# Low weights by an adding transfer, casts on ScalarE and a select for the decay mask in a gated DeltaNet block

## The chip, the cores and the metric

The kernel runs on one core of one Trainium2 chip. The core has five engines that run side by side, each through its own queue in order: TensorE (PE, matrix products), VectorE (DVE), ScalarE (ACT), GpSimd (POOL) and SyncE (SP), which here issues all transfers. The metric is the device time of one execution in microseconds, the median of several; lower is better.

## The reference

One layer of a hybrid block. The input x has 1024 tokens of 1024 channels, and there are 256 context tokens that go through the same weights. Both are normalised and modulated, and one projection `w_in` gives the q, k, v, decay and beta columns of a gated DeltaNet with 8 heads, a gate z for it, and a pooling group with a gate of its own. Both groups are concatenated and go through `w_out`; the result is gated, added to x and normalised.

```
hn = rms_norm(x, gain) * (1 + scale) + shift
proj = hn @ w_in                       # q, k, v | decay, beta | z_dn | u_pool | z_pool
qkv = silu(short_conv(qkv, conv_w))    # 5 taps, centred
decay = exp(where(i >= s, g[i] - g[s], -inf))       # per head, direction and chunk
o_f, s_f = gated_delta_rule(q, k, v, g[0], beta[0], s0_f)      # and backward
o = rms_norm(o_f + flip(o_b)) * silu(z_dn)
y = concat(o, pool_mixer(u_pool) * pool_scale * silu(z_pool))
out = rms_norm(x + gate * (y @ w_out), final_gain)
```

The context is scanned first, and its final states are where the scans of x start. All data is float32.

## The kernel before

**Products in three passes.** TensorE multiplies a rounded format (`FP32R`). To keep float32 accuracy, each factor is split in a high part (a rounded copy) and a low part (the raw value minus the high part), and a product is the sum of high by high, high by low and low by high (`PASSES`, L724). So each tile of weights needs two tiles, `whi` and `wlo`, and each half of the normalised input needs `hnhi` and `hnlo`.

**The tiles of the projection.** `w_in` is worked through in 64 column tiles of 128 columns. A tile is loaded raw (512 KB, `w_load`, L669) into `wraw`, or in turn with a second buffer (tag `kT`) for the first 18 tiles. It is split in two halves of 128 x 512 (`w_split`, L679): ScalarE casts the high half, and GpSimd subtracts it from the raw half to give the low one. `gemm_half` (L734) runs 8 x 3 matmuls for 512 tokens (256 for the context) and, after a fixed number of them, places the split of the next tile and, for the later tiles, the load of the one after. `whi` and `wlo` have two buffers each.

**The stages.** The first 33 us compute the modulation from `w_mod`. Then come 16 context tiles (k and v of 8 heads, 256 columns of moving data each), while `x_half` (L1388) transposes, modulates and splits the input: TensorE transposes into PSUM, ScalarE writes `h32`, VectorE casts it to `hnhi`, and VectorE or GpSimd, in turn, subtracts for `hnlo` (`x_split`, L1408). After them the tiles of the heads (v, k, z, q), two early gates and the pooling columns follow. A tile of q, k or v goes through `conv_post` (L787) on VectorE: four steps for the outer taps, and one after a tanh on ScalarE.

**The jobs.** Two context jobs and eight head jobs go through threads: `stage_d` (L969) loads rows of cumulated decays broadcast over the partitions into the tile `D`, GpSimd adds a mask (0 or -1e30, one 128 x 128 tile per direction, made at the start at L533) and ScalarE takes the exponential. `stage_a` (L990) forms the products of keys, scales them by beta and the decay, and inverts 16 x 16 blocks on VectorE by way of two bounces through DRAM (`ds`, `vs`); `stage_b` merges the inverses, `stage_k`, `stage_q` and `stage_s` prepare the scan, and `scan_ctx` and `scan_x` run it.

**The order of the work.** It is fixed when the program is built, by a planner (`Flow`, L70). The main thread yields after each matmul; the planner keeps an estimated clock for every engine, and puts in a step of a side thread when its estimated due time has come. A thread also waits for flags, such as `("k", k)` when the convolution of a head's keys is written. The cost of each instruction comes from `Engine.cost` (L318), the gaps between engines from the table `AFTER`, and of a transfer from `ISSUE` and `LANDED` (L66). On the chip every engine then takes its instructions in that order and waits on semaphores.

**The end.** From 1023 us on the pooling columns are summed in windows on VectorE (`pool_mix`), split again and multiplied by `pool_w`, whose parts `load_all` (L1744) loads and splits group by group. `second_half` (L1969) frees the pooling tiles and loads the second half of `w_out` and of the mixed output `y`; `out_main` (L1829) contracts them.

Of the kernel before, what the change touches and what calls it, by code (L numbers as in the profile page):

```python
# [8 lines left out]
FP32 = mybir.dt.float32  # L9
# [56 lines left out]
ISSUE = 1220.0  # L66
LANDED = 950.0


# [244 lines left out]
class Engine:  # L314
# [3 lines left out]
    def cost(self, op, a, k):  # L318
# [24 lines left out]
        if op == "tensor_copy":  # L343
            return 80.0 + 3.8 * n
        if op == "memset":
            return 36.0 + 0.83 * n
# [12 lines left out]
    def __getattr__(self, op):  # L359
        f = getattr(self.real, op)  # L360

        def call(*a, **k):
            self.flow.spend(self.name, self.cost(op, a, k), self.uses(op, a, k))
            return f(*a, **k)  # L364

        return call


# [22 lines left out]
def kernel(  # L391
# [90 lines left out]
    ident = const.tile([P, P], FP32, name="ident")  # L482
    mask = [const.tile([P, P], FP32, name=f"mask{d}") for d in range(2)]
    tri = [dl_tile([P, P], "S", 2) for d in range(2)]
# [48 lines left out]
    for d in range(2):  # L533
        pool.memset(mask[d], 0.0)
        pool.memset(tri[d], 1.0)
        s = 1 if d == 0 else -1
        pool.affine_select(out=mask[d], in_=mask[d], pattern=[[s, P]], compare_op=ALU.is_ge, fill=NEG,
                           base=0, channel_multiplier=-s)
        pool.affine_select(out=tri[d], in_=tri[d], pattern=[[s, P]], compare_op=ALU.is_ge, fill=0.0,
                           base=0, channel_multiplier=-s)  # L540
# [138 lines left out]
    def w_split(n, part):  # L679
        if n >= len(order):  # L680
            return
        if part == 0:
            wq[n] = [gemm.tile([P, KT, P], FP32R, tag=f"w{s}", bufs=2, name=f"w{s}") for s in ("hi", "lo")]
        hi, lo = wq[n]
        s = slice(part * (KT // 2), (part + 1) * (KT // 2))
        split(raws[n][:, s, :], hi[:, s, :], lo[:, s, :], dve if n < WD and part else pool)

# [46 lines left out]
    def gemm_half(i, w, src, t0, m, evac):  # L734
        ps = mm_tile()
        j = 0
        for k in range(KT):
            for a, b in PASSES:
                pe.matmul(ps[:, 0:m], w[a][:, k, :], src(b, k, t0),
                          start=(j == 0), stop=(j == 3 * KT - 1))  # L740
                j += 1
                if t0 == 0 and j == (4 if i > 1 else 14) and i:
                    w_split(i + 1, 0)
                if t0 == 0 and j == (14 if i > 1 else 18) and i:
                    w_split(i + 1, 1)
                    if i + 2 >= N2:
                        w_load(i + 2)
                yield
        evac(ps[:, 0:m], t0)
# [219 lines left out]
    def stage_d(J, part):  # L969
# [9 lines left out]
        for d in range(2):  # L979
            pool.tensor_tensor(out=t[:, d], in0=t[:, d], in1=rep(mask[d], 4), op=ALU.add)  # L980
            if d or DY < 8:
# [406 lines left out]
    def x_half(hf):  # L1388
        for k in range(KT):
# [9 lines left out]
            if XACT & 4:  # L1399
# [3 lines left out]
                           scale=md[:, 0, 1, k:k + 1], bias=md[:, 0, 0, k:k + 1])  # L1403
            flow.give()
            flow.flag("h32", n)
            flow.add(x_split(hf, k, h32), [("h32", n)], True)

    def x_split(hf, k, h32):  # L1408
        if XACT & 8:
            yield "dve"  # L1410
        dve.tensor_copy(hn[2 * hf][:, k, :], h32)
        yield
        e = dve if k % XD == 0 else pool
# [70 lines left out]
    def thread_a():  # L1484
# [3 lines left out]
        for k in range(-2, H):  # L1488
            yield ("k", k)
            yield ("ab", k >= 0)  # L1490
            yield ("done", k - 2)
            yield from stage_a(jobs[k])

# [335 lines left out]
    def out_main():  # L1829
# [139 lines left out]
        def second_half():  # L1969
            yield ("mixed",)  # L1970
            pl_p.release()
            pools["c"] = Pool(flow, tc.alloc_tile_pool(name="outc", bufs=1, side="right", reuse_waits="tile"))
# [110 lines left out]
```

## Time and profile before

| | |
|---|---|
| median of 3 runs | 1318.51 us (1318.17 to 1319.07) |
| the profiled execution | 1321.76 us |
| its span, first to last instruction | 1320.0 us |
| TensorE matmul busy | 1212.5 us (92%) |
| VectorE busy | 928.0 us (70%) |
| ScalarE busy | 570.8 us (43%) |
| GpSimd busy | 438.7 us (33%) |
| granted TensorE clock, mean | 0.962 |
| moved by DMA | 123.73 MB |

Busy time is the share of the span in which an engine executes; issuing a transfer does not count as busy. A row of the profile names a line, and nearly all instructions share L364, the line of the recording helper, so rows are told apart by what they write and read: `wlo<-wraw,whi` is the subtraction that makes a low half from the raw and the high half. Behind the shapes stand the count, the busy time in us and the mean of one in ns.

### The profile page before, as it was taken

What the parts mean: (1) busy time and instruction counts of PE and PEld (TensorE: products, weight loads), DVE (VectorE), ACT (ScalarE), POOL (GpSimd) and SP (SyncE); (2) the same over time, 40 slices, a digit from 0 to 9 for tenths busy, and PEclk for the clock granted to TensorE, in tenths of its full rate; (3) what the DMA queues carried; (4) which work ended last, traced back from release to release, by engine and by line L of the source; (5) the groups of instructions that cost most, each with busy time, mean ns of one, the idle gap of its engine ahead of it and who ended that gap; (6) DMA issues with size and microseconds to landing.
All of it is one profiled execution on the core that took longest, in us unless ns stands there. A gap on an engine that the chain in (4) does not pass through costs nothing.

```text
span 1320.0 us, 26398 instructions
## 1 busy us (share of the span) xinstructions
PE 1212.5 (92%) x10631; PEld 977.8 (74%) x10631; DVE 928.0 (70%) x1883; ACT 570.8 (43%) x1498; POOL 438.7 (33%) x451
## 2 busy tenths in 40 slices
PE   8876699899899999999999989999999999799997
PEld 2666577677777877788778768778788777688887
DVE  4799989868886787877776867878433999724212
ACT  3466437444436547455474464643613123322110
POOL 2477433230421423314132233141215454402330
PEclk9788899899999999989999999999999899899999
DMA  9533344223121213212221131212313135565230
GB/s 329 188 99 93 86 140 125 74 57 90 37 49 48 78 42 100 58 46 80 49 83 44 41 100 41 69 63 43 103 60 109 48 104 185 199 206 157 83 112 32
DMA packets 157384, 123.73 MB, mean 94 GB/s; under 512 B 47106, under 2 KB 135115, under 8 KB 157261
## 3 DMA queue, kind: packets, MB, share of 16 engines
q1 hardware_dynamic: 157261, 122.04, 30.6%
q8 instruction: 83, 1.36, 0.4%
q14 instruction: 40, 0.33, 0.1%
HBM read 101.43 MB, written 20.60 MB: 92 GB/s over the span
## 4 chain that ended last, share of the span: by engine, by line
PE 40%; DVE 14%; ACT 6%; DMA 2%; issue 2%; POOL 2%; DVEq 0%; SPq 0%; POOLq 0%; ACTq 0%
PE mm L364 24%; PE sc L364 5%; PE o L364 4%; DVE kT L364 4%; PE pp L364 3%; PE pa L364 3%; DVE t L364 3%; DVE ws L364 3%; ACT junk L364 2%; ACT ks L364 1%; DMA D<-gscr 1%; DVE dlo L364 1%; DVE rp L364 1%; POOL wlo L364 1%; DVE zp L364 1%
## 5 line engine op out<-in xcount | busy, mean ns | idle before, releaser
L364 PE MATMUL mm<-hnhi,whi 128*128 128x512 f32 x768 | 321.0, 418 | 0.9 <-ACT whi L364 0.9
L364 PE MATMUL mm<-hnhi,wlo 128*128 128x512 f32 x768 | 316.7, 412 | 2.0 <-POOL wlo L364 2.0
L364 PE MATMUL mm<-hnlo,whi 128*128 128x512 f32 x768 | 316.9, 413 | 0.0
L364 POOL TENSOR_TENSOR wlo<-wraw,whi 128x512 fp32r<-128x512 f32 x110 | 158.0, 1442 | 337.3 <-ACT whi L364 330.5
L364 PEld LDWEIGHTS mm<-hnhi,whi 128*128 128x128 f32 x768 | 147.7, 192 | 26.8 <-issue 1.7
L364 PEld LDWEIGHTS mm<-hnhi,wlo 128*128 128x128 f32 x768 | 146.9, 191 | 26.0 <-POOL wlo L364 2.5
L364 PEld LDWEIGHTS mm<-hnlo,whi 128*128 128x128 f32 x768 | 147.6, 192 | 22.9
L364 DVE SCALAR_TENSOR_TENSOR kT<-u,cw,kT 128x512 f32<-128x512 f32 (+1 forms) x96 | 94.8, 994 | 5.3 <-ACT kT L364 1.8
L364 POOL TENSOR_TENSOR D<-D,mask 128x512 f32<-128x512 f32 x40 | 58.9, 1478 | 92.3 <-DMA D<-gscr 76.8
L364 ACT ACTIVATE y<-sc 128x256 f32<-128x256 f32 (+1 forms) x65 | 24.9, 383 | 131.3 <-PE sc L364 125.3
L364 ACT ACTIVATE u<-mm 128x512 f32<-128x512 f32 (+1 forms) x64 | 34.8, 543 | 88.3 <-PE mm L364 88.1
L364 DVE SCALAR_TENSOR_TENSOR t<-t,laneN 128x1 f32<-128x1 f32 (+4 forms) x150 | 68.0, 453 | 6.8 <-DMA laneN<-ds 2.8
L364 ACT ACTIVATE whi<-wraw 128x512 fp32r<-128x512 f32 x110 | 67.5, 633 | 1.8 <-DMA wraw<-in_w_in_dram 1.5
L364 DVE SCALAR_TENSOR_TENSOR vT<-u,cw,vT 128x512 f32<-128x512 f32 (+1 forms) x80 | 67.2, 843 | 1.5
L364 DVE TENSOR_TENSOR pw<-mm,zp 128x512 f32<-128x512 f32 (+1 forms) x12 | 8.0, 669 | 83.9 <-PE mm L364 83.9
L364 ACT ACTIVATE D<-D,ngc 128x128 f32<-128x128 f32 x160 | 53.1, 403 | 30.7 <-POOL D L364 30.7
L364 DVE SCALAR_TENSOR_TENSOR qT<-u,cw,qT 128x512 f32<-128x512 f32 (+1 forms) x80 | 63.0, 788 | 2.9 <-ACT qT L364 1.2
L364 DVE SCALAR_TENSOR_TENSOR S<-S,egl,sc 128x128 f32<-128x128 f32 x112 | 33.7, 343 | 33.4 <-PE sc L364 30.4
L364 DVE SCALAR_TENSOR_TENSOR r<-sc,neg,vn 128x128 f32<-128x128 f32 x128 | 38.7, 345 | 23.0 <-PE sc L364 22.9
L364 PEld LDWEIGHTS sc<-S,kT 128*128 128x128 f32 x256 | 36.9, 192 | 15.6 <-issue 9.1
L364 PE MATMUL mm<-D,whi 128*128 128x256 f32 x128 | 41.2, 322 | 7.3 <-DVE ks L364 4.5
L364 PE MATMUL sc<-S,kT 128*128 128x128 f32 x256 | 40.7, 282 | 7.2 <-DVE S L364 6.7
(409 smaller groups left out, 2785.5 us busy)
## 6 DMA issues: line engine op xcount, KB each, us to landing
wraw<-in_w_in_dram SPq DMA_DIRECT2D x55, 512.0 KB, 3.8
D<-gscr SPq DMA_DIRECT2D x40, 256.0 KB, 4.1
qd<-escr SPq DMA_DIRECT2D x16, 512.0 KB
kT<-in_w_in_dram SPq DMA_DIRECT2D x9, 512.0 KB, 4.0
whnhi<-in_w_mod_dram SPq DMA_DIRECT2D x8, 512.0 KB, 3.5
whnlo<-in_w_mod_dram SPq DMA_DIRECT2D x8, 512.0 KB, 9.5
D<-in_w_mod_dram SPq DMA_DIRECT2D x8, 512.0 KB, 4.9
yscr<-zs SPq DMA_DIRECT2D x8, 512.0 KB, 2.8
```

The lines of the kernel that those rows point to most:

```text
L364: return f(*a, **k)
```

## The change

The low half of the weights is made otherwise: ScalarE writes the negated high half into the low tile, and a transfer issued on GpSimd's queue adds the raw half to it. Its cost and landing in the planner are `ADDS` and `ADDED`. For all tiles but the first two, the matmuls run high weights first (16) and then low weights (8), and the splits of the next tile are placed after 2 and 8 matmuls in place of 4 and 14. ScalarE casts `hnhi` from `h32` in place of VectorE. A select on GpSimd sets the masked elements of `D` to -1e30 in place of the addition of a mask tile, and the mask tiles go. `thread_a` waits for the first half of the input before each job, and `second_half` waits for the last group's pooling weights.

```diff
+ADDS = 1000.0
+ADDED = 1500.0
...
+        if op == "affine_select":
+            return 80.0 + 1.7 * n
...
+    def add_to(self, out, in_):
+
+        u = [_use(out, True), _use(in_, False)]
+        self.flow.spend(self.name, ADDS, u)
+        self.flow.note("sync", u, self.flow.free[self.name] + ADDED)
+        return self.real.dma_start(out=out, in_=in_, accum_op=ALU.add)
...
-    mask = [const.tile([P, P], FP32, name=f"mask{d}") for d in range(2)]
...
-        pool.memset(mask[d], 0.0)
...
-        pool.affine_select(out=mask[d], in_=mask[d], pattern=[[s, P]], compare_op=ALU.is_ge, fill=NEG,
-                           base=0, channel_multiplier=-s)
...
-        split(raws[n][:, s, :], hi[:, s, :], lo[:, s, :], dve if n < WD and part else pool)
+        act.activation(out=hi[:, s, :], in_=raws[n][:, s, :], func=ACTF.Copy)
+        act.activation(out=lo[:, s, :], in_=raws[n][:, s, :], func=ACTF.Copy, scale=-1.0)
+        pool.add_to(lo[:, s, :], raws[n][:, s, :])
...
-        for k in range(KT):
-            for a, b in PASSES:
-                pe.matmul(ps[:, 0:m], w[a][:, k, :], src(b, k, t0),
-                          start=(j == 0), stop=(j == 3 * KT - 1))
-                j += 1
-                if t0 == 0 and j == (4 if i > 1 else 14) and i:
-                    w_split(i + 1, 0)
-                if t0 == 0 and j == (14 if i > 1 else 18) and i:
-                    w_split(i + 1, 1)
-                    if i + 2 >= N2:
-                        w_load(i + 2)
-                yield
+        late = [(k, p) for k in range(KT) for p in PASSES[:2]] + [(k, PASSES[2]) for k in range(KT)]
+        for k, (a, b) in late if i > 1 else [(k, p) for k in range(KT) for p in PASSES]:
+            pe.matmul(ps[:, 0:m], w[a][:, k, :], src(b, k, t0),
+                      start=(j == 0), stop=(j == 3 * KT - 1))
+            j += 1
+            if t0 == 0 and j == (2 if i > 1 else 14) and i:
+                w_split(i + 1, 0)
+            if t0 == 0 and j == (8 if i > 1 else 18) and i:
+                w_split(i + 1, 1)
+                if i + 2 >= N2:
+                    w_load(i + 2)
+            yield
...
-            pool.tensor_tensor(out=t[:, d], in0=t[:, d], in1=rep(mask[d], 4), op=ALU.add)
+            s = 1 - 2 * d
+            pool.affine_select(out=t[:, d], in_=t[:, d], pattern=[[0, 4], [s, P]], compare_op=ALU.is_ge, fill=NEG,
+                               base=0, channel_multiplier=-s)
...
+            act.activation(out=hn[2 * hf][:, k, :], in_=h32, func=ACTF.Copy)
             flow.flag("h32", n)
             flow.add(x_split(hf, k, h32), [("h32", n)], True)
+        flow.flag("xt", hf)
...
-        if XACT & 8:
-            yield "dve"
-        dve.tensor_copy(hn[2 * hf][:, k, :], h32)
-        yield
+        yield "pool" if k % XD else "dve"
...
             yield ("done", k - 2)
+            yield ("xt", 0)
             yield from stage_a(jobs[k])
...
             yield ("mixed",)
+            yield ("pw", GROUPS[-1])
             pl_p.release()
```

## Rows read from the trace of the kernel before

**Rows 1.** The windows view, five stages of the span. Columns: the stretch, its length, then for PE, PEld, DVE, ACT and POOL the busy time and the count of instructions, then the granted clock, the DMA engines' mean share and GB/s. The last row sums the stages.

```profile
0.00:33.00 33.00, 27.49 (x78) 6.67 (x79) 13.90 (x41) 9.93 (x22) 8.08 (x28) 1.00 0.94 329
33.00:165.00 132.00, 94.81 (x571) 82.20 (x570) 120.23 (x213) 70.64 (x169) 81.40 (x103) 0.86 0.38 117
165.00:1023.00 858.00, 815.25 (x8771) 663.71 (x8770) 631.15 (x1459) 422.82 (x1205) 256.36 (x258) 0.98 0.25 70
1023.00:1155.00 132.00, 117.04 (x483) 93.93 (x482) 117.97 (x113) 36.51 (x49) 59.07 (x34) 0.94 0.41 134
1155.00:1320.00 165.00, 157.92 (x737) 131.29 (x735) 44.77 (x60) 30.86 (x55) 33.75 (x30) 0.99 0.37 118
sum 1320.00, PE 1212.52 PEld 977.80 DVE 928.03 ACT 570.76 POOL 438.67; mean PE 242.50 PEld 195.56 DVE 185.61 ACT 114.15 POOL 87.73
```

**Rows 2.** The waits of TensorE over the whole span: what waited for what, us in total, times, the longest.

```profile
PE pa L364 <- DVE kT L364: 12.4, 7, 3.6
PE sc L364 <- ACT y L364: 9.2, 6, 2.1
PE pp L364 <- ACT pw L364: 7.1, 1, 7.1
PE mm L364 <- POOL wlo L364: 5.2, 5, 2.0
```

**Rows 3.** Groups of instructions by shape over the whole span, on GpSimd and ScalarE: count, busy us and mean ns of one, then the idle time before them.

```profile
L364 POOL TENSOR_TENSOR wlo<-wraw,whi 128x512 fp32r<-128x512 f32 x110 | 158.0, 1442 | 337.3 <-ACT whi L364 330.5 <-issue 6.7
L364 POOL TENSOR_TENSOR wlo<-kT,whi 128x512 fp32r<-128x512 f32 x18 | 25.1, 1408 | 11.6 <-ACT whi L364 11.6
L364 POOL TENSOR_TENSOR D<-D,mask 128x512 f32<-128x512 f32 x40 | 58.9, 1478 | 92.3 <-DMA D<-gscr 76.8 <-PE sc L364 10.2 <-DVE qd L364 5.3
L364 POOL TENSOR_SCALAR_AFFINE_SELECT t<-t 128x256 f32<-128x256 f32 x10 | 5.5, 545 | 0.7
L364 ACT ACTIVATE whi<-wraw 128x512 fp32r<-128x512 f32 x110 | 67.5, 633 | 1.8 <-DMA wraw<-in_w_in_dram 1.5
```

**Rows 4.** Groups by shape on VectorE between 33 and 165 us, in the same columns.

```profile
L364 DVE SCALAR_TENSOR_TENSOR kT<-u,cw,kT 128x256 f32<-128x256 f32 x30 | 19.4, 648 | 2.5 <-ACT kT L364 1.8
L364 DVE SCALAR_TENSOR_TENSOR vT<-u,cw,vT 128x256 f32<-128x256 f32 x16 | 15.3, 956 | 0.4
...
L364 DVE CAST hnhi<-XT 128x512 fp32r<-128x512 f32 x4 | 6.2, 1554 | 0.0
...
L364 DVE CAST hnhi<-tmp 128x512 fp32r<-128x512 f32 x4 | 4.0, 1003 | 0.2 <-ACT tmp L364 0.2
...
L364 DVE CAST hnhi<-W 128x512 fp32r<-128x512 f32 x4 | 2.7, 683 | 0.0
...
L364 DVE CAST hnhi<-Y 128x512 fp32r<-128x512 f32 x4 | 2.6, 638 | 0.0
...
L364 DVE SCALAR_TENSOR_TENSOR vT<-u,vT 128x256 f32<-128x256 f32 x4 | 1.7, 416 | 0.0
```

**Rows 5.** Groups by shape on GpSimd between 33 and 165 us.

```profile
L364 POOL TENSOR_TENSOR wlo<-wraw,whi 128x512 fp32r<-128x512 f32 x17 | 23.7, 1402 | 19.7 <-ACT whi L364 19.7
L364 POOL TENSOR_TENSOR wlo<-kT,whi 128x512 fp32r<-128x512 f32 x16 | 22.4, 1409 | 3.2 <-ACT whi L364 3.2
```

**Rows 6.** The timeline between 60 and 76 us: start, duration in us, engine, operation. The two matmuls are neighbours in a context tile.

```profile
65.40 1.29 POOL L364 TENSOR_TENSOR wlo<-wraw,whi 128x512 fp32r<-128x512 f32 x1 [2.43 <-ACT whi L364]
65.45 1.34 DVE L364 TENSOR_SCALAR ngc<-y 128x32 f32<-128x32 f32 x1
...
66.00 0.28 PE L364 MATMUL mm<-zs,whi 128*128 128x256 f32 x1
66.12 0.29 PE L364 MATMUL mm<-D,wlo 128*128 128x256 f32 x1
```

**Rows 7.** GpSimd's timeline between 1018 and 1095 us, the first and the last of the four pairs of subtractions that lie together (the others are at 1058.87 and 1073.03).

```profile
1039.17 4.14 POOL L364 TENSOR_TENSOR wlo<-wraw,whi 128x512 fp32r<-128x512 f32 x2 [4.65 <-ACT whi L364]
...
1091.97 3.53 POOL L364 TENSOR_TENSOR wlo<-wraw,whi 128x512 fp32r<-128x512 f32 x2 [14.20 <-ACT whi L364]
```

**Rows 8.** Groups by shape on VectorE over the whole span: the same subtraction of 1024 elements in two places.

```profile
L364 DVE TENSOR_TENSOR dlo<-ws,dhi 128x1024 fp32r<-128x1024 f32 x8 | 17.0, 2122 | 2.2 <-ACT dhi L364 2.2
...
L364 DVE TENSOR_TENSOR dlo<-zp,dhi 128x1024 fp32r<-128x1024 f32 x2 | 2.4, 1224 | 0.6 <-ACT dhi L364 0.6
```

**Rows 9.** DMA issues over the whole span (count, KB each, median us from issue to landing), and one issue in SP's timeline.

```profile
D<-gscr SPq DMA_DIRECT2D x40, 256.0 KB, 4.1
...
yscr<-zs SPq DMA_DIRECT2D x8, 512.0 KB, 2.8
...
66.71 0.37 SPq L382 DMA_DIRECT2D wraw<-in_w_in_dram  x1
```

**Rows 10.** ScalarE's timeline between 1095 and 1160 us, the cast of the last pooling weights and the one before it.

```profile
1143.29 1.06 ACT L364 ACTIVATE wohi<-outa 128x1024 fp32r<-128x1024 f32 x1 [0.30 <-DMA outa<-in_w_out_dram]
1144.25 0.61 ACT L364 ACTIVATE pw<-pwr 128x512 fp32r<-128x512 f32 x1
```

**Rows 11.** Timelines of TensorE and ScalarE: the first product of the first context job, and the conversion of the eighth input tile.

```profile
96.51 1.06 PE L364 MATMUL pa<-kT 128*128 128x128 f32 x8
...
104.60 0.77 ACT L364 ACTIVATE Y<-pp,md 128x512 f32<-128x512 f32 x1
```

**Rows 12.** The waits of SP's queue over the whole span, the largest.

```profile
SPq L382 <- POOL wlo L364: 406.6, 40, 24.8
```

## The prediction

> **What bounds the kernel now.** I read the windows of five stages first, then TensorE's waits, then the groups by shape, and last the timelines of the two stages in which TensorE idles most. TensorE is busy 1212.5 of 1320.0 us, so 107.5 us is the most that less waiting can bring [rows 1]. It is spread unevenly: from 33 to 165 us TensorE works 94.8 of 132 us while VectorE works 120.2, 91% of the stage; from 165 to 1023 TensorE idles 42.8 of 858; from 1023 to 1155 it idles 15.0 of 132 beside a VectorE at 118.0; the last stage is TensorE's own [rows 1]. In the first and the fourth stage VectorE sets the pace.
>
> VectorE does not work all of that time. A cast of 512 elements takes 0.64 to 1.55 us by the tile it reads; the convolution step of 256 elements takes 0.65 or 0.96 us in the mean and 0.42 in its undisturbed form [rows 4]. The timeline shows why: an operation of 32 elements lasts 1.34 us, and beside it GpSimd's low-weight subtraction runs for 1.29 us, ending within 0.1 us of it [rows 6]. While GpSimd subtracts, VectorE's instruction stands. TensorE itself hardly waits for the low weights (5.2 us in all) [rows 2].
>
> **The change part by part.** All sums are against the profiled execution, 1321.76 us (span 1320.0 and 1.76 around it); it is 3.25 us above the median 1318.51 of the plain runs, so I take the differences over to the median.
>
> Low weights. 128 subtractions on GpSimd go (110 at 1.44 and 18 at 1.41 us, 183 us) [rows 3]. In their place come 128 ScalarE copies at about 0.63 us, the row of the high cast (81 us), and 128 transfer issues on GpSimd. No row shows such an issue. From below it is SP's issue, 0.37 us [rows 9]; from above the subtraction it replaces, 1.44. I take 1.0, the middle. No row shows the landing of an adding transfer; plain ones land in 2.8 us (512 KB) and 4.1 us (256 KB) [rows 9]; I take 4.1, the same size. On the DMA engines 33 transfers of 256 KB in the first stage are 8.4 MB, 64 GB/s beside the 117 there at a share of 0.38 [rows 1]; at the same price a byte the share goes to 0.59, and to 0.8 if adding costs double, so room is left.
>
> First stage, 33 to 165. Of VectorE's time the 16 casts go, 6.2 + 4.0 + 2.7 + 2.6 = 15.5 us; the listed convolution steps stand above their undisturbed 0.42 by 30 x 0.23 + 16 x 0.54 = 15.5 us [rows 4], and GpSimd's 33 low-weight operations, 46.1 us, are more than half of its 81.4 in the stage [rows 1, 5], so I take half to two thirds of that away. VectorE falls to about 120.2 - 15.5 - 9 = 96, less where its small operations were held too. ScalarE then takes its place: 70.6 us now, and 33 low copies and 16 casts at 0.63 us, 31 us, make 101.5. If ScalarE could be as full as VectorE is today (91%), the stage would take 111 us; if nothing moved, 132. ScalarE sits between producers and consumers and waits on both, so I take the middle, 121.5: **-10.5 us** (0 to -30.5, the last at ScalarE fully busy).
>
> The new wait of the first context job for the first half of the input. In the trace the eighth conversion of that half starts at 104.60 us and the first product of that job at 96.51 [rows 11]: at the old pace the wait would hold it 8 us, at a pace 8% faster and without VectorE's casts about nothing. Behind the wait stand only that thread's own instructions. I take 0, with +8 as the other end.
>
> Does a context tile get its low weights in time? Now the first half is issued at matmul 2 of one tile and first read at matmul 17 of the next: 24 - 2 + 16 = 38 matmuls. They follow each other at 0.12 us [rows 6], 4.6 us bare, but 16 tiles in about 132 us make 8 us a tile, 13 us of lead. The chain is 2 x 0.63 + 1.0 + 4.1 = 6.4 us. Hidden, except for the first three tiles, which start from an empty pipe or keep the old order of passes: **+2 us** (0 to 6).
>
> Heads, 165 to 1023. The first product of each head's job waits for VectorE's convolution of kT (12.4 us in 7 waits) and the scan for ScalarE's y (9.2 us in 6) [rows 2]. The first is VectorE late behind GpSimd's subtractions, masks and decayed queries; the queries stay, so I take half of it: **-6 us**. The mask becomes a select over 512 elements: 40 additions at 1.48 us against twice the 256-element select, 1.09 us at most [rows 3], so 16 us less on GpSimd, off TensorE's path; beside the y wait I book 0. ScalarE gains 0.63 us per half tile; it is busy 422.8 of 858 [rows 1] and has the room. Range 0 to -21.6, and +5 if its copies get in front of ks and y.
>
> Pooling stage, 1023 to 1155. Four pairs of subtractions lie beside VectorE's chain there; each pair takes 3.5 to 4.1 us or more [rows 7] against 2.6 for two like the one of 1.29 us [rows 6], and the additions of 1024 elements take 2.12 us in the mean where an undisturbed one takes 1.22 [rows 8]. Eight subtractions that hold VectorE for up to 1.29 us each are 10.3 us; one pair is partly beside TensorE's own work: **-8 us** (-3 to -10). The transfer of the output weights' low parts is not changed, so that contention stays.
>
> The wait for the last pooling weights before the second half's loads. TensorE stands 7.1 us until ScalarE has cast pw [rows 2]; the cast runs at 1144.25 behind a cast of output weights that starts at 1143.29 [rows 10]. With the wait the pw load goes ahead of those loads: about half, **-3 us** (0 to -7). The delayed loads are for the second half of the contraction, behind 32 us of products of the first; hidden.
>
> New order of passes: the same 24 matmuls, 0. Mask tiles at the start: 0; TensorE waits there for the first loads anyway.
>
> Sum: -10.5 + 2 - 6 - 8 - 3 = **-25.5 us**, 1296.3 for a profiled run, **1293 us** at the median.
>
> SBUF — State Buffer of the Trainium skill, section "Who interferes with whom", puts the rule behind the 1.34 us row: two-input VectorE work and a GpSimd instruction that reads SBUF exclude each other for a whole instruction. The trace agrees. Its section "A bandwidth-pool intuition that's wrong" speaks against the change: a GpSimd-issued transfer of about 0.62 us took 3.1 us beside a VectorE copy, because its descriptors could not be written; 128 times the 2.5 us between would be some 320 us of GpSimd (an estimate). No row here shows it; the third rival has its like from rows.
>
> **The rivals.**
> 1. ScalarE bounds the first stage outright, or the context jobs' own chain does: the stage keeps 132 us. For it: ScalarE goes from 70.6 to 101.5 us. Against: even so it has 30 us free. Sum -25.5 + 10.5 = -15: 1303.5 us.
> 2. Slower: the raw buffer comes free later, and SP, in order, stands on it. SP waits for wlo 406.6 us in 40 waits, up to 24.8 [rows 12]. A half was free 0.63 + 1.44 = 2.1 us after its split began; now after 1.26 + (0.37 to 1.44) + (2.8 to 4.1) = 4.4 to 6.8. The second half's split moves six matmuls up, at least 6 x 0.12 = 0.7. Net 1.6 to 4.0 us a tile. If two transfers of each head's chain (the decay rows, the small-inverse bounce) stand behind such a wait, 8 x 2 x 4.0 = 64 us: 1318.5 - 25.5 + 64 = 1357; at 1.6 us it is even (25.6 against 25.5), so it decides from there. Against: today's 406.6 us of such waits already delay TensorE little, so mostly nothing urgent stands behind.
> 3. The issue is held by VectorE: GpSimd stays the blocked side. The like in the trace is a held subtraction, whose pairs reach 4.1 us [rows 7]; with 3.4 us an issue the first stage's GpSimd is 33 x 3.4 + 81.4 - 46.1 = 147 us, over the 132: +15 in place of -10.5, sum 0, about 1318.5. Against: the casts, which could do it, leave VectorE.
>
> **How the numbers follow.** Forecast 0.61 (own range 1278 to 1308), rival 1 0.16, rival 2 0.13, rival 3 0.10. Less than 0.2%, 2.6 us, can't be told from no change. Faster: 0.61 + 0.16 + 0.02 of rival 3 = 0.79; same 0.05; slower 0.13 + 0.03 = 0.16. The range reaches from 1268, where the first stage and the heads' waits give most of their bounds (-50), to 1321, which takes in rivals 1 and 3 and leaves out rival 2.
>
> **What would show it.** Right: VectorE's 256-element convolution steps near 0.42 us in the first stage and its busy time there at 96 us or less; ScalarE near 101; no wait of PE mm for the adding transfers beyond the first tiles; DVE additions near 1.22 us between 1039 and 1095; the pw wait of 7.1 us at half. Wrong: PE mm waiting for wlo's transfer in most tiles; SP's waits on it with D or laneN late behind; a first stage as long as before; GpSimd's issues so long that the selects and powers come late.

## The result and the profile after

The changed kernel takes 1336.32 us (median of four runs, 1333.49 to 1339.05) against 1318.34 for the kernel before: a ratio of 1.0136, 95% interval 1.0111 to 1.0161. It is 1.4% slower. The forecast was 1293.0 with a range up to 1321, so the time lies outside the range, on the side that had a chance of 0.16. The profiled execution took 1334.72 us.

The windows of the same five stages, in the columns of [rows 1]:

```profile
0.00:33.00 33.00, 27.47 (x78) 6.78 (x79) 13.93 (x45) 9.95 (x23) 6.64 (x23) 1.00 0.95 330
33.00:165.00 132.00, 82.66 (x459) 70.28 (x457) 61.86 (x149) 77.84 (x170) 46.20 (x88) 0.79 0.68 158
165.00:1023.00 858.00, 810.58 (x8798) 661.26 (x8796) 622.97 (x1492) 480.32 (x1323) 186.70 (x255) 0.98 0.40 96
1023.00:1155.00 132.00, 123.13 (x511) 99.42 (x511) 112.94 (x117) 45.70 (x70) 51.41 (x52) 0.94 0.54 150
1155.00:1333.00 178.00, 170.78 (x793) 141.88 (x791) 51.40 (x67) 34.91 (x60) 37.83 (x32) 0.99 0.41 132
```

Between 33 and 165 us VectorE fell from 120.2 us of work to 61.9, and yet TensorE got less done, 82.7 us in place of 94.8. Part of VectorE's fall is work that has moved behind 165 us because the stage is late: up to 195 us, just behind the first gate (the product whose store leaves at 161 us before and 191 after), it works 79.3 us. Even so it is idle for half of that time, and the stage is slower. The DMA engines are busy for 0.68 of the stage in place of 0.38.

TensorE's waits, to be held against [rows 2]:

```profile
PE mm L368 <- DMA wlo<-wraw: 24.5, 11, 4.9
PE pp L368 <- ACT W L368: 11.2, 2, 10.3
PE pa L368 <- DVE kT L368: 9.5, 7, 4.2
...
PE mm L368 <- DMA wlo<-kT: 6.8, 4, 2.7
...
PE pp L368 <- DVE pw L368: 1.1, 1, 1.1
```

The 5.2 us of waiting for GpSimd's low weights have become 31.3 us of waiting for transfers that land, in 15 waits, and 27.1 us of them lie between 33 and 195 us. The wait of 7.1 us for ScalarE's cast of the pooling weights is gone; the one on VectorE's part of them, the last row, is 1.1 us (3.0 before).

The wait of 10.3 us for ScalarE's `W` is new (0.6 us before in all). `W` is one of the four temporaries through which the input is converted. GpSimd's subtraction from one filling of it runs 39 us after the cast that it follows; ScalarE fills it again only behind that, and TensorE's transposes wait for ScalarE:

```profile
106.87 0.63 ACT L368 ACTIVATE hnhi<-W 128x512 fp32r<-128x512 f32 x1
145.66 1.42 POOL L368 TENSOR_TENSOR hnlo<-W,hnhi 128x512 fp32r<-128x512 f32 x1
148.61 0.76 ACT L368 ACTIVATE W<-pp,md 128x512 f32<-128x512 f32 x1
149.42 1.12 PE L368 MATMUL pp<-ident,B 128*128 128x128 f32 x4 [10.29 <-ACT W L368]
```

ScalarE does not stand for the subtraction itself: it works on the context job's norms and decays up to 148.6 us. So by this view the wait comes from the place of the step in ScalarE's order.

Groups by shape, GpSimd's and ScalarE's, beside [rows 3]; then the page's DMA queues and one row of the DMA issues (count, KB each, median us from issue to landing):

```profile
L377 POOL DMA_DIRECT2D wlo<-wraw x110 | 98.6, 902 | 496.6 <-ACT wlo L368 323.9 <-PE pp L368 73.9 <-DVE sm L368 73.0
L368 POOL TENSOR_SCALAR_AFFINE_SELECT D<-D 128x512 f32<-128x512 f32 x40 | 36.2, 987 | 14.4 <-DMA D<-gscr 14.4
...
L368 ACT ACTIVATE wlo<-wraw 128x512 fp32r<-128x512 f32 x110 | 68.6, 623 | 0.0
```

```profile
q1 hardware_dynamic: 157261, 122.04, 30.4%
q0 software_dynamic: 18432, 33.56, 14.7%
...
wlo<-wraw POOLq DMA_DIRECT2D x110, 256.0 KB, 3.7
```

The single prices came out near what was estimated: the issue 0.90 us (1.0 taken), the landing 3.7 (4.1 taken), the copy 0.62 (0.63), the select 0.99 (1.09 at most). What they do to the order of events is in the chain of waits between 62 and 95 us (start, us, what):

```profile
66.94 5.69 DMA wraw<-in_w_in_dram
...
72.71 0.04 ACT whi L368
...
73.25 0.61 ACT wlo L368
...
74.65 0.34 ACT wlo L368
...
75.46 3.69 DMA wlo<-wraw
...
79.27 5.73 DMA wraw<-in_w_in_dram
```

One raw buffer goes round in 12.3 us: load, casts, issue and landing, next load. Two such buffers give two tiles in 12.3 us. That alone is no slower than before, when loads into `wraw` left 10 to 17 us apart between 54 and 124 us; what the held buffer costs is measured below (*h2*). TensorE's timeline shows the other end of the same loop:

```profile
77.63 0.74 PE L368 MATMUL mm<-D,wlo 128*128 128x256 f32 x4 [1.72 <-DMA wlo<-wraw]
79.19 0.98 PE L368 MATMUL mm<-D,wlo 128*128 128x256 f32 x4 [0.83 <-DMA wlo<-wraw]
79.97 0.42 PE L368 MATMUL mm<-D,whi 128*128 128x256 f32 x1
80.19 0.41 PE L368 MATMUL mm<-zs,whi 128*128 128x256 f32 x1
80.40 0.41 PE L368 MATMUL mm<-D,whi 128*128 128x256 f32 x1
```

It waits for the low weights of both halves, and the matmuls after that follow each other at 0.21 us where [rows 6] has 0.12: from 80 to 82.5 us the granted clock is 0.50, 1.2 of 2.4 GHz, after TensorE had worked 0.74 of the 2 us from 77 to 79. The mean of the stage is 0.79, 0.86 before.

Marks in SP's timeline tell where in the execution the time goes: the store of the first gate, the outputs of the first and the seventh head, and the last store of the output.

| kernel | first gate | first head | seventh head | last store |
|---|---|---|---|---|
| before | 161 | 425 | 942 | 1316 |
| after | 191 | 454 | 960 | 1329 |

The loss is 30 us by the first gate and 29 at the first head. Six heads then win 11 back (84.3 us a head, 86.2 before), and the pooling and output stages 5 more. That is near the forecast's total for heads and pooling (17 us); its first stage went wrong by some 40 us.

### The profile page after: what moved, and what is told of

Its sections match the earlier page's. It is cut to its first block, busy times and chain, and to the rows that moved or that the text cites. A ratio compares the mean times of both kernels' runs of the same rounds, so it can differ in the third digit from the quotient of the medians.

```text
span 1333.0 us, 26734 instructions
## 1 busy us (share of the span) xinstructions
PE 1214.6 (91%) x10631; PEld 979.6 (73%) x10631; DVE 863.1 (65%) x1867; ACT 648.7 (49%) x1642; POOL 328.8 (25%) x447
## 3 DMA queue, kind: packets, MB, share of 16 engines
q1 hardware_dynamic: 157261, 122.04, 30.4%
q0 software_dynamic: 18432, 33.56, 14.7%
## 4 chain that ended last, share of the span: by engine, by line
PE 56%; DVE 18%; ACT 13%; DMA 7%; issue 4%; POOL 2%; DVEq 0%; ACTq 0%; SPq 0%; POOLq 0%
PE mm L368 33%; PE sc L368 7%; PE o L368 6%; PE pp L368 6%; DVE t L368 6%; DVE kT L368 5%; PE pa L368 4%; ACT junk L368 3%; DMA wlo<-wraw 2%; DMA wraw<-in_w_in_dram 2%; ACT u L368 1%; ACT wlo L368 1%; ACT ks L368 1%; ACT whi L368 1%; ACT B L368 1%
## 5 line engine op out<-in xcount | busy, mean ns | idle before, releaser
L368 PE MATMUL mm<-hnhi,wlo 128*128 128x512 f32 x768 | 230.6, 413 | 0.4 <-issue 0.4
L377 POOL DMA_DIRECT2D wlo<-wraw x110 | 98.6, 902 | 496.6 <-ACT wlo L368 323.9
L368 PEld LDWEIGHTS mm<-hnhi,wlo 128*128 128x128 f32 x768 | 137.3, 190 | 23.1 <-issue 1.4
L368 DVE SCALAR_TENSOR_TENSOR kT<-u,cw,kT 128x512 f32<-128x512 f32 (+1 forms) x96 | 100.9, 1052 | 15.3 <-ACT kT L368 11.3
L368 ACT ACTIVATE wlo<-wraw 128x512 fp32r<-128x512 f32 x110 | 68.6, 623 | 0.0
L368 DVE SCALAR_TENSOR_TENSOR t<-t,laneN 128x1 f32<-128x1 f32 (+4 forms) x150 | 55.2, 368 | 8.4 <-DMA laneN<-ds 4.2
L368 DVE SCALAR_TENSOR_TENSOR vT<-u,cw,vT 128x512 f32<-128x512 f32 (+1 forms) x80 | 58.3, 728 | 2.1 <-ACT vT L368 0.7
L368 PE MATMUL mm<-D,wlo 128*128 128x256 f32 x128 | 30.8, 351 | 31.3 <-DMA wlo<-wraw 24.5
L368 DVE SCALAR_TENSOR_TENSOR qT<-u,cw,qT 128x512 f32<-128x512 f32 (+1 forms) x80 | 56.0, 702 | 4.6 <-ACT qT L368 2.4
```

Of the source, the lines that this page charges most:

```text
L377: return self.real.dma_start(out=out, in_=in_, accum_op=ALU.add)
```

## The experiments

**Same order, other operation.** The planner lays out every engine's order from the costs that it is told. So the chip's operation can be changed while the planner is told another, and the order stays. Four kernels: *e2*, everything of the change, but all low weights by subtraction, planner told so; *e9*, that order with the transfers; *after*; and *e10*, after's order with subtractions. *e1* has subtractions for the 16 context tiles alone.

```diff
# e2 (e1: only where n < 16)
-        act.activation(out=hi[:, s, :], in_=raws[n][:, s, :], func=ACTF.Copy)
-        act.activation(out=lo[:, s, :], in_=raws[n][:, s, :], func=ACTF.Copy, scale=-1.0)
-        pool.add_to(lo[:, s, :], raws[n][:, s, :])
+        split(raws[n][:, s, :], hi[:, s, :], lo[:, s, :], pool)
...
# e10: told the transfer, done as a subtraction (e9 the reverse)
...
+        flow.spend("act", act.cost("activation", (), k), act.uses("activation", (), k))
...
+        flow.spend("pool", ADDS, u)
+        flow.note("sync", u, flow.free["pool"] + ADDED)
+        pool.real.tensor_tensor(out=l, in0=r, in1=h, op=ALU.subtract)
```

> The changed kernel, but the low weights of the 16 context tiles come from GpSimd's subtraction again; the other 48 tiles keep the transfer. In the changed kernel the first gate's store is issued at 191 us against 161 before, while the six head periods between the stores from the first head to the seventh take 505.6 us against 517.3. Loop theory (two raw buffers, each held from its load until the adding transfer has landed) and order theory (the planner, which takes the transfer as cheap, puts the input's conversion late) both expect the first gate's store at 150 to 165 us and the head periods still near 506: 1290 to 1305 us. A theory that ScalarE's copies cost the time everywhere expects little: above 1325.

> The changed kernel with GpSimd's subtraction for all low weights; the casts on ScalarE, the select, the new pass order and the two waits stay. Loop and order theory: first gate's store at 150 to 165 us, head periods 510 to 517 us in all, pooling stage as before: 1303 to 1316 us. If one of the other parts is what costs (the wait of the context jobs, the casts), the store stays near 190 and the time above 1330.

> The order of work is that of the kernel with the subtraction everywhere (the planner is told of the subtraction), but the chip does the negated copy and the adding transfer. Loop theory: the wait for the landing holds the raw buffers here as well; first gate's store later than in the subtraction kernel by 15 us or more, time at least 15 us above it. Order theory: store within 5 us of the subtraction kernel's, time equal or lower.

> The order of work is that of the changed kernel (the planner is told of the copy and the transfer), but the chip does the subtraction on GpSimd. Loop theory: raw buffers come free 2 to 5 us a tile earlier; first gate's store at 165 us or before, time at or below 1318. Order theory: the input's conversion stands as late in the queues as in the changed kernel, store at 180 us or later, time 1325 or more.

| kernel | order made for | done as | time | ratio, interval | first gate | first head | seventh head |
|---|---|---|---|---|---|---|---|
| after | transfers | transfers | 1336.3 | 1.0136 (1.0111 to 1.0161) | 191 | 454 | 960 |
| e10 | transfers | subtractions | 1330.9 | 1.0100 (1.0074 to 1.0126) | 171 | 437 | 951 |
| e2 | subtractions | subtractions | 1335.5 | 1.0137 (1.0103 to 1.0172) | 167 | 441 | 953 |
| e9 | subtractions | transfers | 1387.5 | 1.0527 (1.0473 to 1.0582) | 193 | 486 | 1013 |
| e1 | mixed | mixed | 1314.4 | 0.9979 (0.9961 to 0.9997) | 167 | 435 | 937 |

In one and the same order the transfers cost 20 us (after against e10) or 26 us (e9 against e2) up to the first gate. In the heads they win 8 us in an order made for them (506 us for six heads against 514) and lose 15 in one that is not. So the transfers explain 20 of the 30 us of the first stage, and over the whole kernel, in after's order, 5 us net (1336.3 against 1330.9). e9 came out as its loop theory expected, 15 us or more later than e2. But e1, e2 and e10 missed what was expected of them: with all subtractions the time is still 13 to 18 us above the kernel before (1317.3 in these runs), and e1 is 3 us below it where 12 to 27 were expected. Something else in the change costs more than the transfers do. In e10 it is there early: 10 us at the first gate, 12 at the first head, 9 at the seventh, 10 at the last store. The wait for `W` stands in e10 too:

```profile
PE pp L368 <- ACT W L368: 14.2, 2, 13.3
```

**A theory that was not confirmed: the input's subtraction is placed too late.** In e2 two of GpSimd's input subtractions ran 17 and 26 us after their casts, and the temporaries that they held were filled again only behind them. In the change that step is placed when the planner's GpSimd is free. *f2*, *f1* and *f4* are e2, after and e1 with it placed at once; *f3* is the kernel before with only the conversion's part of the change.

```diff
-        yield "pool" if k % XD else "dve"
+        yield None if k % XD else "dve"
```

> All low weights by subtraction, and GpSimd's input subtraction is placed as soon as its cast is (plain yield), not when the planner's GpSimd is free. Theory 'held subtraction': in e2 two of GpSimd's input subtractions ran 26 us after their casts and kept the temporaries W and Y from the next conversions; with the plain place all 16 conversions lie between about 76 and 135 us, the first gate's store goes out by 160 us, and the time is 1308 to 1320. Rival 'the wait of the job for the first half': the first job, not the conversion, sets the stage; the time stays at 1330 to 1340. Rival 'pass order and split places': also 1330 to 1340, with the head period still near 86 us.

> The changed kernel whole, transfers included, with the plain place alone. Theory 'held subtraction' and theory 'raw-buffer loop' add up: the loop (load, cast, issue, landing through two raw buffers, some 12 us for two tiles) stays, so the first stage still ends 10 to 20 us late; time 1318 to 1328. If the held subtraction is all: 1300 to 1312. If it is nothing: 1333 to 1340.

> Plain place, subtraction for the 16 context tiles and transfers from there on (e1 with the plain place). Theory 'held subtraction': e1's first gate store (167) comes to 155 to 162, and of its 1314.4 go 5 to 12: 1302 to 1310. Rival: no change from e1, 1312 to 1318.

> The kernel before with the conversion's part alone: ScalarE's cast, GpSimd's subtraction placed when the planner's GpSimd is free, and the job's wait for the first half (without that wait this order can't run to its end). Theory 'held subtraction': slower than before by most of e2's 18 us, 1328 to 1342, with GpSimd's input subtractions long after their casts. Rival 'pass order, split places, select': within 5 of before, 1313 to 1323.

Measured: f2 1326.3 (e2 less 9), f1 1368.0 (after plus 32), f4 1323.8 (e1 plus 9), f3 1322.3, a ratio of 1.0030 (1.0015 to 1.0045). The same line moves the time by -9, +32 and +9 us, and the first gate's store of f2 came later (173 for 167), not at 160. In f2 the wait for `W` is down to 2.7 us, but others came in its place (8.2 us for VectorE's `ks`, 7.4 for a transfer into `laneN`), so the early place did not bring the stage forward. In f3 the wait is there (9.8 us), the first gate comes at 165, and the whole costs 3 us. The late step is thus seen in the traces, but its price was not separated: no run moved that step with the rest of the order kept. What f1, f2 and f4 show is how much the time hangs on the order: one step moved, and all that the planner lays out after it moves.

**Which parts, and from which tile.** *g6* leaves the first 16 tiles as before and takes the transfers, the pass order, the select and the pooling wait from there on; *g8* is g6 with subtractions; *g7* is e1 with the old order of passes and places in the context tiles; *e3* is after with the context tiles' raw half added from DRAM, so that the transfer does not hold the raw buffer.

```diff
# g6, g7, g8 (what all three share here)
...
-        for k, (a, b) in late if i > 1 else ...
-            if t0 == 0 and j == (2 if i > 1 else 14) and i:
+        for k, (a, b) in late if i > 15 else ...
+            if t0 == 0 and j == (2 if i > 15 else 4 if i > 1 else 14) and i:
...
# e3
-        pool.add_to(lo[:, s, :], raws[n][:, s, :])
+        pool.add_to(lo[:, s, :], w_in_d[:, s, order[n]:order[n] + P] if n < 16 else raws[n][:, s, :])
```

> The kernel before up to its 16 context tiles (subtraction, VectorE's casts of the input, old places of the splits, no wait of the job), and from tile 16 on the change: transfers, new pass order and places, select, wait for the pooling weights. Theory 'all of the loss lies in the first stage': the first gate's store stays at 159 to 163, the heads give about 12 and the pooling stage 5 to 7: 1298 to 1306. Rival 'the heads' gain was only catching up': 1314 to 1322.

> The same with subtractions in place of all transfers. If the transfers are what the heads gain from: 1312 to 1321, some 10 above the run with them. If the new pass order, the select and the wait give it: within 4 of that run.

> e1 (subtraction for the context tiles, ScalarE's cast, the job's wait) with the old pass order and split places for the context tiles. Theory 'the early places push the context tiles ahead of the conversion': the last conversion comes from 150 to 145 or less, the first gate's store from 167 to 160 to 165, the time to 1302 to 1310. Theory 'the conversion alone': no change, 1311 to 1318.

> The changed kernel, but the transfers of the context tiles add the raw half from w_in in DRAM, so that the raw buffer is free after ScalarE's two casts. Theory 'raw-buffer loop': the loads follow each other sooner than 12 us for two tiles, and the first gate's store comes from 191 to 165 to 175: 1314 to 1324. Rival 'landing and contention of the transfers themselves': no more than 5 earlier, 1330 to 1337.

Measured: g6 1367.7, g8 1335.2, g7 1372.4, e3 1362.4; the ratios' intervals lie within 1.0097 and 1.0460. All missed. In g6 and g8 the first gate is stored at 153 and 156, sooner than before, and the first head comes out at 434 and 443, later than before; g6 then needs 91 us a head. So the heads can lose by themselves, with the first stage in good order. In e3 the first gate stays at 192: TensorE waits 36.0 us for the transfers, which land in 7.4 us from DRAM:

```profile
wlo<-in_w_in_dram POOLq DMA_DIRECT2D x32, 256.0 KB, 7.4
```

Since the landing doubled, e3 can't tell what freeing the raw buffer is worth.

**What of the transfer costs the first stage.** Three kernels in after's order, with e10's subtractions (first gate 171), that add for each half of the 16 context tiles one transfer issued on GpSimd behind the subtraction, each made to carry one property: *h1* the traffic alone (256 KB a half from `w_in` to a spare tensor in DRAM), *h2* the held raw buffer alone (512 bytes out of the raw half), *h3* the landing alone (64 bytes of zeros added to the low half).

```diff
...
+        pool.real.tensor_tensor(out=l, in0=r, in1=h, op=ALU.subtract)
+        if n < 16:
+            # h1
+            pool.real.dma_start(out=spare[n, part], in_=w_in_d[:, s, order[n]:order[n] + P], accum_op=ALU.add)
+            # h2
+            pool.real.dma_start(out=spare[n, part:part + 1, :], in_=raws[n][0:1, 4 * part, :])
+            # h3
+            pool.real.dma_start(out=lo[0:1, 4 * part, 0:16], in_=nil, accum_op=ALU.add)
```

> Order and subtractions of the run in which the changed kernel's order is kept and GpSimd subtracts (first gate store 171), and for each half of the 16 context tiles an adding transfer of 256 KB more, from w_in into a spare DRAM tensor: traffic like the change's, but no one waits for it and no buffer is held by it. Theory 'traffic': the DMA engines' share from 66 to 132 us rises from 0.35 to 0.8 or more, the loads land later, and the gate's store comes at 183 to 193. Rival 'hold and landing': store at 171 to 176.

> The same order with subtractions, and for each half of the context tiles a transfer of 512 bytes from the raw half into a spare tensor, issued on GpSimd behind the subtraction: the raw buffer is held for issue and landing as in the change, with no traffic. Theory 'raw buffer held': gate store at 183 to 193. Rivals 'traffic' and 'low weights late': 171 to 176.

> The same order with subtractions, and for each half of the context tiles an adding transfer of 64 bytes of zeros into the low half: the matmuls wait for issue and landing as in the change, the raw buffer is free after the subtraction, and there is no traffic. Theory 'low weights late': gate store at 183 to 193 with TensorE's waits for the transfer near the change's 31 us. Rivals: 171 to 176.

| kernel | added to e10 | 14th context tile | first gate | time |
|---|---|---|---|---|
| before | | 134 | 161 | 1318.3 |
| e10 | nothing | 114 | 171 | 1330.9 |
| h2 | raw buffer held | 119 | 178 | 1337.8 |
| h1 | traffic | 130 | 188 | 1346.0 |
| h3 | landing of 64 bytes | 139 | 192 | 1346.9 |
| after | the real transfer (for the subtraction) | 139 | 191 | 1336.3 |

The third column is the end of the 14th context tile in TensorE's timeline; the first gate's tile comes next in all of them. h3, with the landing and without the traffic, comes out where after does. The row of TensorE's waits between 33 and 195 us in h3, and its DMA issue:

```profile
PE mm L368 <- DMA wlo<-nil: 26.6, 12, 4.0
```

```profile
wlo<-nil POOLq DMA_DIRECT2D x32, 0.1 KB, 3.6
```

26.6 us of waiting for 64 bytes, against 27.1 for 256 KB in the same window of after, and a landing of 3.6 us against 3.7: the size hardly matters. But h3 is not the landing alone. Its subtraction of 1.4 us stands where the change has a copy of 0.62 on another engine, and each half also costs GpSimd an issue. These rows are of 33 to 165 us, in h3, h2 and h1:

```profile
L704 POOL DMA_DIRECT2D wlo<-nil x30 | 24.1, 803 | 8.8 <-POOL wlo L702 8.8
L703 POOL DMA_DIRECT2D spare<-wraw x16 | 9.1, 566 | 0.0
L703 POOL DMA_DIRECT2D spare<-in_w_in_dram x30 | 48.6, 1647 | 0.0
```

h2 has the subtractions too, with issues of 0.57 us in place of 0.80, and its TensorE waits 1.8 us between 33 and 195 us for low weights; issues and held buffer together cost it 7 us, and h3 lies 14 us beyond it. So the landing is the larger part of h3's 21 us, and its exact share is not known. h1 shows that traffic can cost as much, but not at after's amount. The window of 66 to 132 us has a DMA share of 1.02 there (last but one column), 0.85 in after and 0.35 in e10, and the issue holds GpSimd for 1.65 us a half. The windows of h1, after and e10:

```profile
66.00:132.00 66.00, 45.05 (x295) 41.84 (x294) 59.15 (x67) 34.89 (x82) 55.38 (x68) 0.83 1.02 170
66.00:132.00 66.00, 42.42 (x270) 38.67 (x271) 31.66 (x69) 44.41 (x100) 22.83 (x50) 0.89 0.85 176
66.00:132.00 66.00, 42.66 (x299) 41.00 (x299) 54.94 (x73) 42.64 (x99) 41.72 (x58) 0.81 0.35 96
```

The third column tells one thing more. After's order puts the context tiles early: with subtractions (e10) the 14th is done 20 us sooner than before, and yet the gate behind it comes 57 us later, where before it took 27. The transfers use up that lead, and after's tiles end only 5 us later than before's. The other 25 us of the first gate's delay lie between that tile and the gate; 10.3 of them are the wait for `W`, and the rest was not taken apart.

**Where the other 13 to 18 us are.** *h4* is the kernel before with the new pass order and split places alone, from tile 16 on, laid out anew by the planner: every engine does the same number of instructions on the same data as before. *h5* has the new pass order with every engine's order kept; *h6* has the select in place of the 40 mask additions, every engine's order kept.

```diff
# h5: told the old pass, done the new one
...
+                flow.spend("pe", pe.cost("matmul", (), told), pe.uses("matmul", (), told))
+                k1, (a1, b1) = late[j] if i > 15 else (k, (a, b))
+                pe.real.matmul(ps[:, 0:m], w[a1][:, k1, :], src(b1, k1, t0),
...
# h6: told the addition, done the select
...
+            flow.spend("pool", pool.cost("tensor_tensor", (), told), pool.uses("tensor_tensor", (), told))
+            pool.real.affine_select(out=t[:, d], in_=t[:, d], pattern=[[0, 4], [s, P]], compare_op=ALU.is_ge,
+                                    fill=NEG, base=0, channel_multiplier=-s)
```

> The kernel before with the new pass order and split places alone, from tile 16 on. Theory 'the planner's order of the heads is what moves by +-20 us, whatever the edit': the first gate's store at 161 and the first head's output at 435 to 445 in place of 425; 1325 to 1340. Rival 'the order costs nothing': 1314 to 1322.

> The kernel before with every engine's order kept as it is; only the 24 matmuls of a tile, from tile 16 on, run high weights first and low weights last. Theory 'the planner's new order of the heads, not the parts, costs the rest': within 5 us of before, 1313 to 1323, and the first head's output at 420 to 430. Rival 'the pass order itself stalls TensorE' (the changed order of the whole gave 1360): 1335 or more.

> The kernel before with every engine's order kept and the 40 mask additions on GpSimd (1.48 us) replaced by the select. Theory 'the parts are each harmless or good in a kept order': 1310 to 1319, faster by 0 to 8. Rival 'the select costs the time': 1324 or more.

| kernel | time | ratio, interval | first gate | first head | seventh head |
|---|---|---|---|---|---|
| before | 1318.3 | 1 | 161 | 425 | 942 |
| h4, new passes and places, order laid out anew | 1360.2 | 1.0306 (1.0284 to 1.0328) | 161 | 446 | 981 |
| h5, new passes, order kept | 1316.4 | 0.9992 (0.9978 to 1.0005) | 160 | 422 | 934 |
| h6, select, order kept | 1286.2 | 0.9765 (0.9745 to 0.9786) | 154 | 417 | 909 |

The pass order by itself is worth nothing that can be told from zero. The same instructions with the splits placed earlier, in the order that the planner makes around that, cost 41 us; the earlier splits and the new layout were not told apart. And the select, which the forecast had booked at 0, is worth 33 us (28 to 34 by the interval) when the order is left alone: h6 beats both kernels by over 2%. Its rows, GpSimd's group, then VectorE's steps of the key convolution (between 165 and 1023 us) before, in h6, in h4 and in after:

```profile
L983 POOL TENSOR_SCALAR_AFFINE_SELECT D<-D 128x512 f32<-128x512 f32 x40 | 32.5, 814 | 90.5 <-DMA D<-gscr 85.3 <-PE sc L364 5.2
```

```profile
L364 DVE SCALAR_TENSOR_TENSOR kT<-u,cw,kT 128x512 f32<-128x512 f32 x64 | 74.4, 1172 | 2.6
L364 DVE SCALAR_TENSOR_TENSOR kT<-u,cw,kT 128x512 f32<-128x512 f32 x64 | 61.6, 971 | 2.6
L364 DVE SCALAR_TENSOR_TENSOR kT<-u,cw,kT 128x512 f32<-128x512 f32 x64 | 61.8, 972 | 2.1
L368 DVE SCALAR_TENSOR_TENSOR kT<-u,cw,kT 128x512 f32<-128x512 f32 x64 | 85.4, 1336 | 2.8
```

and the waits that they feed: in h6 TensorE's for the keys (12.4 us in [rows 2]), then ScalarE's for the masked decays, before and in h6:

```profile
PE pa L364 <- DVE kT L364: 3.6, 1, 3.6
```

```profile
ACT D L364 <- POOL D L364: 30.7, 13, 7.8
ACT D L364 <- POOL D L983: 18.9, 12, 4.1
```

The select is shorter (0.81 us for 1.48), VectorE's steps are 0.20 us shorter in h6 than before, and the two waits at which a head's job starts both shrink. How much of the 33 us comes from the shorter GpSimd step and how much from VectorE being held less was not separated. The shorter VectorE step is not a sign of the select by itself: h4 has it with the additions, and after, with the select, has the longest.

## Why the prediction was wrong

**The bound of the first stage.** Right in what it saw, wrong in what followed. VectorE's held steps did go: its 256-element convolution steps fell from 0.65 and 0.96 us [rows 4] to

```profile
L368 DVE SCALAR_TENSOR_TENSOR kT<-u,cw,kT 128x256 f32<-128x256 f32 x28 | 13.6, 484 | 10.8 <-ACT kT L368 9.8
L368 DVE SCALAR_TENSOR_TENSOR vT<-u,cw,vT 128x256 f32<-128x256 f32 x16 | 8.9, 556 | 1.2 <-ACT vT L368 0.7
```

and its work up to the first gate from 120.2 to 79.3 us (96 forecast). ScalarE came to 98.2 us up to there (101.5 forecast). The stage did not follow either, so the step "-10.5" failed: 30 us later at the first gate. One sentence on it is off: the rule quoted from the Trainium skill is for VectorE work with two inputs, and the row of 1.34 us that it was set behind (`ngc<-y`) has one.

**"Does a context tile get its low weights in time? ... Hidden".** This is the step that failed first. The lead of 13 us took 38 matmuls at 8 us a tile, as if a tile's split began at matmul 2 of the tile before and tiles were spread evenly. In the chain above the split begins when the raw half lands, at 72.6 us, and that load had left only when the adding transfer of two tiles before had landed. Tiles come in pairs, and TensorE stands ready for the low weights at 75.9 us (77.63 less its wait of 1.72): a lead of 3.3 us, less even than the forecast's bare 4.6 for the 38 matmuls, against a chain of 6.4. The 6.4 us of the chain were near (0.6 + 0.6 + 0.9 + 3.7 is 5.8; in the chain above 6.5 from the landing of the raw half to that of the low one); the lead was not there. The price up to the first gate is 20 to 26 us, where 2 stood; the landing has the larger part of it in h3, and how the rest divides between held buffer and traffic stays open. On the landing, the Trainium skill, "DMA: Bandwidth & Descriptors", section "Anatomy of one DMA — SWDGE (gpsimd) path", gives a transfer issued by GpSimd a fixed 2.0 us plus its bytes at 436 GB/s, an estimate of 2.6 us for 256 KB of which most does not depend on size. The trace agrees on that (3.6 us for 64 bytes, 3.7 for 256 KB), not on the amount.

**DMA engines, "so room is left".** The share in the stage came to 0.68, between the 0.59 and 0.8 that were worked out, but 0.85 from 66 to 132 us. h1 shows that traffic is not free at 1.02; whether it is at 0.85 no run shows.

**Heads -6, pooling -8, pooling weights -3.** After is 11 us faster over six heads and about 5 from there to the end; in its order the transfers win 8 and 6 of that (e10: 375 us from the seventh head to the last store, after: 369). The sum of 17 was about right, but not by the reasons given, so that is luck. The wait for `kT` fell by 2.9 us and not by 6 (12.4 to 9.5), and VectorE's steps of 512 elements in the heads became longer, 1.34 us for 1.17, although GpSimd's subtractions were gone. The VectorE steps of 1024 elements in the pooling stage fell from 2.12 to 1.47 us, and as far in e10, which subtracts. The wait of 7.1 us for the pooling weights went altogether; what that won was not measured alone.

**The mask, "beside the y wait I book 0".** In the order of before, this term is off by 33 us, in the kernel's favour. The select's 16 us on GpSimd were taken as off TensorE's path, and [rows 2] has no wait of TensorE for GpSimd's `D`. ScalarE has one (30.7 us), and [rows 2] names VectorE's `kT`; of that wait the forecast put half down to the low weights and masks together and gave the select nothing. In after the gain does not show: e10 has the select and needs 514 us for six heads, before 517, h6 491.

**"New order of passes: 0".** Right for the passes (h5), and blind to the rest. All terms were added as if each engine's order stayed as it was. The change hands the planner other costs, other flags and other places, and it lays out all the work anew. h4 shows that this can cost 41 us with no instruction added. It does not show what it costs in after: h4 loses nothing up to the first gate (161), 21 us from there to the first head and 18 in the six heads, while e10, with the subtractions, has lost 10 us at the first gate and 12 at the first head and needs no more than before for the six heads. So the 13 to 18 us that remain beside the transfers lie in the main before the first head. The wait for `W` stands there; what else moved, and what it costs, stays open, and so does why the select's gain is missing in after's order.

**The rivals.** None had the mechanism. Rival 2 had the late raw buffer, but put its harm in the heads behind SP, whose waits on `wlo` did grow (643.2 us in 53 waits, against [rows 12]); h2 prices the held buffer, with its issues, at 7 us, in the first stage. Rival 3 was rightly held unlikely: an issue took 0.90 us, not 3.4.

## What to carry to other kernels

Where a program lays out the order, measure each part of a change first with the order held fixed; here two parts in the old order were worth 0 and -33 us, and a new order of the same instructions +41, so a sum over parts says little until the order is part of it. A transfer put in place of an engine's instruction has to be priced by its landing at the point where its result is read, and not by its bytes alone: the kernel with 64 bytes had its first gate at 192 us, the one with 256 KB at 191. The time that is left until that point is to be read from where the instructions lie in the trace, and not from their mean spacing. Emptying a full engine shortens a stage only if nothing else in it is late: here VectorE lost a third of its work and the stage grew.

## What was not expected of the hardware

An adding transfer of 64 bytes issued on GpSimd landed in 3.6 us, one of 256 KB in 3.7, and one of 256 KB from DRAM in 7.4. The adding transfers took the DMA engines 14.7% of the span for 33.56 MB, 0.44% a MB, against 0.25% for the plain ones (30.4% for 122.04 MB), 1.75 times as much; memories and packet sizes differ too, so that adding alone is the reason is not shown. The select over 512 elements took 0.81 us in h6 and 0.99 in after, where two of 256 would have been 1.09.
